# Taking the float32 splits of weights and tokens off GpSimd in a two-layer trunk

## The chip, the cores and the metric

The kernel runs on one core of one Trainium2 chip. The metric is the device time of one execution in microseconds (us); a kernel is described by the median of several executions. One more execution is taken with the hardware profiler, and every duration below comes from that one. TensorE is PE in the rows, VectorE DVE, ScalarE ACT, GpSimd POOL, SyncE SP.

## The reference, cut to what matters

Two trunk layers, each followed by a SwiGLU feed-forward. Layer 0 mixes tokens by latent attention (MLA) and by gated linear attention (GLA) side by side; layer 1 is a convolution module with 31 taps and a layer norm. There are 1152 tokens of width 1024, all in float32.

```python
def modulate(x, g, shift, scale):          # ahead of every sub-layer
    return rmsnorm(x, g) * (1 + scale) + shift

def ffn(h):                                # after every layer, hidden width 2816
    return (silu(h @ w_gate) * (h @ w_up)) @ w_down

# gla_scan, per chunk: q, k scaled by exp of the cumulated log decay
o = scores @ v + (q * exp(cum)) @ state
# conv module: h @ w_pw1, GLU, depthwise 31 taps, layernorm, silu, @ w_pw2
```

## The kernel before

Tokens lie along the free axis, features on the 128 partitions. The tokens form four tiles of 280 to 296 columns; tiles 0 and 1 make the group GA, tiles 2 and 3 the group GB, and the stages of the two groups are interleaved so that one group's feed-forward (the matmuls) covers the other group's convolution or norm.

**Splits.** TensorE takes a rounded float32 (fp32r). To keep the accuracy each operand is held as H, a rounded copy, and L, the rest. `split` (L155) makes H by a ScalarE copy (L156) and then L = source - H (L157), on VectorE unless another engine is given. `mm3` (L159) then spends three matmuls on a product: H of the weight by H of the token tile (L161), H by L (L162), L of the weight by H (L163). The last needs the weight's L, `wL`, the second the token tile's, `hL`.

**Weights.** `wtile` (L412) takes three buffers each of `wraw`, `wH` and `wL`, starts the load on SP's queue and splits it. A weight tile is 128x1024 for gate, up and the convolution's products, and 128x512 or narrower for w_down. The counter `self.wn` and the stage's entry of `WPOOL = (0, 3, 3, 0, 0)` send every third weight tile's L to GpSimd in two kinds of stage: in GA's first feed-forward, and from the moment the convolution's taps are queued (`conv_taps`, L1275) until the layer norm that follows.

**Tokens.** `affine` (L375), the last step of `modulate`, has two forms that alternate over the 8 blocks of 128 features. One uses ScalarE and VectorE directly (L390, L391); the other is `mode` 1, which multiplies on VectorE (L381), applies shift and scale on ScalarE (L383) and splits with L on GpSimd (L384). `layer_norm` splits its odd blocks with L on GpSimd (L1305). Ahead of `affine`, `x_stats` sums squares on VectorE (`ssum`, L373), and TensorE turns the sum into a row for all partitions (L188).

**Linear attention.** In `gla_b` ScalarE writes exponentials into a tile `kq` for two halves f of the heads (L904, L911). Each `kq` is then multiplied by `gqk` in two parts: the first (L913, 128x896) on VectorE for f = 0 and on GpSimd for f = 1, the second (L915, 128x1152) on VectorE for both. TensorE reads the products at L928.

**Beside it.** The convolution's taps are 31 dependent multiply-adds of some 575 or 592 columns for each of 8 blocks and each group, all on VectorE. They are pinned in their own order and dripped a few at a time between feed-forward tiles. VectorE also multiplies the gate product (`ev`, L448), splits it (`aL`), adds the result to x (L409), and sums the conditioning rows (`ada`, L292). Attention's probabilities are split with L (`pL`) on GpSimd for every fourth key block (L1233).

**Order.** A tile scheduler decides each engine's program order from the dependences and its own costs; then each engine runs its queue strictly in order.

Of the kernel before, what the change touches and what calls it, by code (L numbers as in the profile page):

```python
# [18 lines left out]
P = 128  # L19
# [12 lines left out]
W_STEP = 18  # L32
QA, Q0, Q_STEP = 3, 1, 6
FOLD = 512
WPOOL = (0, 3, 3, 0, 0)
A2 = 60
AK, MODS0 = 6, (0, 1) * 3 + (0, 0)
WB = 3, 3, 3
# [29 lines left out]
def segs(tt, w):  # L68
    return [(0, P, 0), (P, w, 1)] if tt == 0 else [(0, w, 1)]
# [47 lines left out]
class Trunk:  # L117
    def __init__(self, tc, A, O):
        self.tc, self.nc, self.A, self.O = tc, tc.nc, A, O
        self.n = 0  # L120
        self.ps = None
        self.pend = deque()
        self.ada_bank = "m"
        self.wn = self.wpool = 0
        self.sw = 512
        self.ada_pin = False
        self.adq = self.nc.sync
# [248 lines left out]
    def affine(self, tt, k, x, bc, H, L, sh, a, mode):  # L376
        nc = self.nc
        w = x.shape[1]
        if mode:
            u, y = self.tmp()[:, :w], self.tmp()[:, :w]  # L380
            nc.vector.tensor_mul(u, x, bc)  # L381
            for s, e, g in segs(tt, w):
                nc.scalar.activation(y[:, s:e], u[:, s:e], AF.Identity, bias=sh[:, k, g:g + 1], scale=a[:, k, g:g + 1])  # L383
            self.split(H[:, k, :], L[:, k, :], y, nc.gpsimd)  # L384
            return
        t = self.tmp()[:, :w]
        for s, e, g in segs(tt, w):
            nc.vector.scalar_tensor_tensor(t[:, s:e], x[:, s:e], a[:, k, g:g + 1], bc[:, s:e],
                                           op0=ALU.mult, op1=ALU.mult)
            nc.scalar.activation(H[:, k, s:e], t[:, s:e], AF.Identity, bias=sh[:, k, g:g + 1])  # L390
            nc.vector.scalar_tensor_tensor(L[:, k, s:e], t[:, s:e], sh[:, k, g:g + 1], H[:, k, s:e].bitcast(F32),  # L391
                                           op0=ALU.add, op1=ALU.subtract)
# [17 lines left out]
                                                X[tt][:, o, s:e], op0=ALU.mult, op1=ALU.add)  # L410

    def wtile(self, src):  # L412
        self.wn += 1
        eng = self.nc.gpsimd if self.wpool and self.wn % self.wpool == 0 else None
        n = src.shape[1]
        raw = self.t(self.wp, [P, KD, P], "wraw", WB[0])[:, :n]
        self.nc.sync.dma_start(raw, src)
        H = self.t(self.wp, [P, KD, P], "wH", WB[1], F32R)[:, :n]
        L = self.t(self.wp, [P, KD, P], "wL", WB[2], F32R)[:, :n]
        self.split(H, L, raw, eng)  # L420
        return H, L

    def drip(self, n):
# [132 lines left out]
    def layer0_mix(self):  # L556
        nc, A, tc = self.nc, self.A, self.tc
# [175 lines left out]
            X.update(xs)  # L733
            self.xg = getattr(self, "xg", []) + [x]
        hs = {}
        self.wpool = WPOOL[0]
        for grp in (GA, GB):
            if grp is GB:
                mx = {tt: self.h_tiles(tt, T1[tt][1] - T1[tt][0]) for tt in GB}
# [133 lines left out]
    def gla_b(self, t):  # L873
        nc, kg, S, tb = self.nc, self.kg, self.S, self.gb
        fs, bs = kg[:, 0:1024], kg[:, 1024:2048]
        NL = len(LEVELS)
        tok = slice(t * P, (t + 1) * P)
        gqk = self.t(tb, [P, 4, P], "gqk", 2)
# [12 lines left out]
        for f in range(2):  # L891
            kq = self.t(tb, [P, 2 * NL + 2, P], "kq", 3)
            for d in range(2):
                src = fs if d == 0 else bs
                for half in range(2):
                    E = self.bank("g")
                    for i, L in enumerate((laH, laL)):
                        nc.tensor.matmul(E, L[:, d * 256 + f * P:d * 256 + (f + 1) * P],
                                         src[:, half * 512:half * 512 + 512], start=(i == 0), stop=(i == 1))
                    for q in range(4):  # L900
                        l = half * 4 + q
                        iv = E[:, q * P:(q + 1) * P]
                        if l == NL:
                            nc.scalar.activation(kq[:, 2 * NL + d, :], iv, AF.Exp)  # L904
                            continue
                        s = LEVELS[l]
                        base = kq[:, l, :] if d == 0 else kq[:, l, s:]
                        st = NL * P + s if d == 0 else NL * P - s
                        ov = bass.AP(base.tensor, base.offset,
                                     [list(base.ap[0]), [st, 2], [2 * s, 64 // s], [1, s]])  # L910
                        nc.scalar.activation(ov, iv.rearrange("p (a b c) -> p a b c", a=2, c=s), AF.Exp)  # L911
                    yield
            (nc.gpsimd if f else nc.vector).tensor_mul(kq[:, 0:NL], kq[:, 0:NL], gqk[:, f, :].unsqueeze(1).to_broadcast([P, NL, P]))  # L913
            yield
            nc.vector.tensor_mul(kq[:, NL:], kq[:, NL:],  # L915
                                 gqk[:, 2 + f, :].unsqueeze(1).to_broadcast([P, NL + 2, P]))
            KQ.append(kq)
            yield
# [341 lines left out]
    def conv_taps(self, u, f, outs):  # L1260
        nc = self.nc
        n = outs[-1][1] + outs[-1][0].shape[1]
        ys, pin = [], self.tc.keep_in_program_order

        def tap(i):
            c = self.cvw[:, f, i:i + 1]
            if i == 0:
                ys.append(self.t(self.up, [P, max(UA, UB) - 2 * CPAD], "y")[:, :n])
            y = ys[0]
            if i == 0:  # L1270
                pin(nc.vector.tensor_scalar(y, u[:, 0:n], c, self.b_dw[:, f:f + 1], op0=ALU.mult, op1=ALU.add))
            else:
                for d, o in outs if i == CW - 1 else [(y, 0)]:
                    w = d.shape[1]
                    pin(nc.vector.scalar_tensor_tensor(d, u[:, i + o:i + o + w], c, y[:, o:o + w],  # L1275
                                                       op0=ALU.mult, op1=ALU.add))
        self.pend.extend(lambda i=i: tap(i) for i in range(CW))
        self.wpool = WPOOL[2]

    def layer_norm(self, C, tts):  # L1280
        nc = self.nc
        us = {}
        for tt in tts:
            c = C[tt]
            w = c.shape[2]
            ssum = self.t(self.tp, [P, self.sw], "ssum", 2)[:, :w]
            nc.vector.tensor_add(ssum, c[:, 0], c[:, 1])
            for f in range(2, KD):
                nc.vector.tensor_add(ssum, ssum, c[:, f])
            mu = self.bank()[:, :w]  # L1290
            nc.tensor.matmul(mu, self.onesd, ssum, start=True, stop=True)
            s2 = self.t(self.tp, [P, self.sw], "ssum", 2)[:, :w]
            for f in range(KD):
                nc.vector.tensor_sub(c[:, f], c[:, f], mu)
                sq = s2 if f == 0 else self.tmp()[:, :w]
                nc.scalar.activation(sq, c[:, f], AF.Square)
                if f:
                    nc.vector.tensor_add(s2, s2, sq)
            bc = self.bcast_rstd(s2, w)
            H, L = self.h_tiles(tt, w)  # L1300
            for f in range(KD):
                y = self.tmp()[:, :w]
                nc.vector.tensor_mul(y, c[:, f], bc)
                nc.scalar.activation(y, y, AF.Silu, bias=self.ln_b[:, f:f + 1], scale=self.ln_g[:, f:f + 1])
                self.split(H[:, f], L[:, f], y, nc.gpsimd if f % 2 else nc.vector)  # L1305
            us[tt] = (H, L)
        return us

# [44 lines left out]
    def layers(self, X, hs):  # L1353
        nc, A = self.nc, self.A
        pa = self.pool("act")
        self.wpool = WPOOL[1]
        NB = max(C0A + C0B + C1A + C1B)
        cut = lambda ns: list(zip(np.cumsum((0,) + ns).tolist(), ns))
        chunks = cut(C0A)
# [12 lines left out]
            if f0 == chunks[1][0]:  # L1372
                hs.update(self.modulate(X, 0, 1, GB))
        self.adp.release()
        self.wpool = 0
        gate = self.par[1][2]
        nc.vector.tensor_mul(self.bg, gate, self.b_pw2.unsqueeze(2).to_broadcast([P, KD, 2]))
        w2 = A["conv_w_pw2"][0].rearrange("(k p) f -> p k f", p=P)
# [8 lines left out]
        for c in chunks[1:-1]:  # L1387
            self.ffn(X, hs, 0, GB, *c, pa, NB, R_FF0)
        self.drip(10 ** 6)
        self.wpool = WPOOL[3]  # L1390
        us = self.layer_norm(C, GA)
        self.ffn(X, hs, 0, GB, *chunks[-1], pa, NB)
        X2 = {}
# [8 lines left out]
        for c in chunks[:-2]:  # L1402
            self.ffn(X2, h2, 1, GA, *c, pa, NB, R_FF1)
        self.drip(10 ** 6)
        self.wpool = WPOOL[3]
        us = self.layer_norm(C, GB)
        self.x_load(X2, GB)
        self.ffn(X2, h2, 1, GA, *chunks[-2], pa, NB)
# [1 line left out]
        h2.update(self.modulate(X2, 1, 1, GB))  # L1410
        self.ffn(X2, h2, 1, GA, *chunks[-1], pa, NB)
        self.store_y(X2, GA)
        self.wpool = WPOOL[4]
        self.up.release()
        for c in cut(C1B):
            self.ffn(X2, h2, 1, GB, *c, pa, NB)
# [57 lines left out]
```

## Time and profile before

| | |
|---|---|
| median of 3 executions | 3096.03 us (3094.78 to 3100.07) |
| the profiled execution, its own time | 3098.96 us |
| its span in the trace | 3097.2 us |
| TensorE busy | 97% of the span |
| VectorE busy | 70% |
| ScalarE busy | 40% |
| GpSimd busy | 13% |
| mean granted TensorE clock | 0.984 |

The span is the time between the first and the last traced instruction; 1.8 us of the profiled execution lie outside it. Where TensorE is busy all the time, only an instruction that TensorE has to wait for can change the end.

### The profile page before, as it was taken

To read this page: it belongs to the slowest core of one execution; us is meant where nothing else is said; L and a number is where in the kernel's file an instruction comes from. 1 tells how busy PE (TensorE), PEld (TensorE's weight loads), DVE (VectorE), ACT (ScalarE), POOL (GpSimd) and SP (SyncE) were. 2 spreads that over 40 slices of the span, in tenths; PEclk is the share of its full clock that TensorE was granted. 3 is DMA by queue.
4 is the path that set the end of the run, shared out by engine and by line. 5 is a ranking of instruction groups with operands and counts; after the bars stand their busy time and mean duration, and the time that the engine had idled before them with its cause. 6 is when DMAs were issued, how large, how long until landed. Compare 5 with 4: busy or idle time off the path is not lost.

```text
span 3097.2 us, 53660 instructions
## 1 busy us (share of the span) xinstructions
PE 3002.1 (97%) x21044; PEld 2813.7 (91%) x21044; DVE 2169.4 (70%) x4110; ACT 1232.1 (40%) x2652; POOL 405.2 (13%) x371
## 2 busy tenths in 40 slices
PE   7999999999989999999999999999999999999999
PEld 4999866666769999999999999999999999999998
DVE  6668478788769999634679996667888875433343
ACT  5323377566664333223422223562222255222222
POOL 1012121112120111111111110111111010000000
PEclk9999999999999999999999999999999999999999
DMA  7545522111164555423232222522322231322222
GB/s 266 169 120 149 156 88 70 55 46 52 26 188 151 168 157 155 127 82 103 80 86 83 78 82 76 149 69 83 89 86 86 83 113 51 110 82 83 81 86 78
DMA packets 449631, 320.46 MB, mean 103 GB/s; under 512 B 29646, under 2 KB 413907, under 8 KB 449378
## 3 DMA queue, kind: packets, MB, share of 16 engines
q1 hardware_dynamic: 411726, 271.06, 29.3%
q0 software_dynamic: 8944, 30.68, 3.1%
q10 hardware_dynamic: 28708, 15.29, 1.7%
q8 instruction: 166, 2.72, 0.4%
q14 instruction: 87, 0.71, 0.1%
HBM read 278.30 MB, written 38.67 MB: 102 GB/s over the span
## 4 chain that ended last, share of the span: by engine, by line
PE 75%; DVE 13%; ACT 5%; DMA 3%; issue 3%; POOL 0%; SPq 0%; ACTq 0%; DVEq 0%; POOLq 0%
PE ps_a L161 16%; PE ps_a L163 16%; PE ps_a L162 16%; PE ps_d L162 3%; PE ps_d L163 3%; PE ps_d L161 3%; DVE y L1275 2%; PE ps_g L928 2%; PE ps_a L538 2%; PE ps_a L540 2%; PE ps_a L539 2%; DVE ada L292 1%; DVE wL L157 1%; DVE x L409 1%; PE ps_c L1236 1%
## 5 line engine op out<-in xcount | busy, mean ns | idle before, releaser
L163 PE MATMUL ps_a<-hH,wL 128*128 128x288 f32 (+2 forms) x3328 | 985.3, 296 | 6.7 <-DVE wL L157 6.7
L161 PE MATMUL ps_a<-hH,wH 128*128 128x288 f32 (+2 forms) x3328 | 983.9, 296 | 1.8 <-ACT wH L156 1.8
L162 PE MATMUL ps_a<-hL,wH 128*128 128x288 f32 (+2 forms) x3328 | 985.2, 296 | 0.0
L156 ACT CAST wH<-wraw 128x1024 fp32r<-128x1024 f32 (+3 forms) x432 | 362.4, 843 | 768.4 <-PE ps_a L162 480.7
L163 PEld LDWEIGHTS ps_a<-hH,wL 128*128 128x128 f32 x3328 | 627.7, 189 | 8.0 <-DVE wL L157 7.8
L161 PEld LDWEIGHTS ps_a<-hH,wH 128*128 128x128 f32 x3328 | 629.0, 189 | 2.6 <-ACT wH L156 2.3
L162 PEld LDWEIGHTS ps_a<-hL,wH 128*128 128x128 f32 x3328 | 627.5, 189 | 0.2
L157 DVE TENSOR_TENSOR wL<-wraw,wH 128x1024 fp32r<-128x1024 f32 (+3 forms) x349 | 336.0, 965 | 130.2 <-ACT wH L156 129.3
L1275 DVE SCALAR_TENSOR_TENSOR y<-u,cvw,y 128x575 f32<-128x575 f32 (+1 forms) x464 | 420.1, 905 | 8.4
L157 POOL TENSOR_TENSOR wL<-wraw,wH 128x1024 fp32r<-128x1024 f32 (+2 forms) x83 | 172.7, 2081 | 975.3 <-ACT wH L156 975.1
L161 PE MATMUL ps_a<-aH,wH 128*128 128x288 f32 (+2 forms) x880 | 259.8, 296 | 0.2 <-ACT wH L156 0.2
L163 PE MATMUL ps_a<-aH,wL 128*128 128x288 f32 (+2 forms) x880 | 259.0, 295 | 0.0
L162 PE MATMUL ps_a<-aL,wH 128*128 128x288 f32 (+2 forms) x880 | 258.9, 294 | 0.0
L448 DVE TENSOR_TENSOR ev<-ev,ps_a 128x288 f32<-128x288 f32 (+2 forms) x176 | 79.3, 450 | 226.9 <-PE ps_a L163 225.6
L292 DVE SCALAR_TENSOR_TENSOR ada<-ada,scc,ada 128x512 f32<-128x512 f32 (+1 forms) x364 | 219.7, 647 | 20.0 <-DMA ada<-in_w_ada 19.8
L156 ACT CAST aH<-ev 128x288 fp32r<-128x288 f32 (+2 forms) x176 | 75.9, 431 | 330.7 <-DVE ev L448 329.1
L161 PEld LDWEIGHTS ps_a<-aH,wH 128*128 128x128 f32 x880 | 165.9, 189 | 0.5 <-ACT wH L156 0.5
L162 PEld LDWEIGHTS ps_a<-aL,wH 128*128 128x128 f32 x880 | 166.1, 189 | 0.0
L163 PEld LDWEIGHTS ps_a<-aH,wL 128*128 128x128 f32 x880 | 165.5, 188 | 0.5 <-DVE wL L157 0.5
L161 PE MATMUL ps_d<-aH,wH 128*128 128x288 f32 (+2 forms) x528 | 158.3, 300 | 6.3 <-ACT wH L156 3.5
L161 PE MATMUL ps_d<-hH,wH 128*128 128x288 f32 (+2 forms) x512 | 153.2, 299 | 8.6 <-DVE dr L1248 6.6
L409 DVE SCALAR_TENSOR_TENSOR x<-ps_a,par,x 128x288 f32<-128x288 f32 (+5 forms) x300 | 128.5, 450 | 45.8 <-PE ps_a L163 45.1
(338 smaller groups left out, 5770.7 us busy)
## 6 DMA issues: line engine op xcount, KB each, us to landing
wraw<-in_ffn_w_gate SPq DMA_DIRECT2D x88, 512.0 KB
wraw<-in_ffn_w_up SPq DMA_DIRECT2D x88, 512.0 KB
wraw<-in_ffn_w_down SPq DMA_DIRECT2D x144, 256.0 KB
ada<-in_w_ada SPq DMA_DIRECT2D x112, 256.0 KB
wraw<-in_conv_w_pw SPq DMA_DIRECT2D x48, 512.0 KB
in<-in_w_ada SPq DMA_DIRECT2D x8, 1024.0 KB
ada<-in_w_ada SPq DMA_DIRECT2D x64, 128.0 KB
wraw<-in_w_out SPq DMA_DIRECT2D x16, 512.0 KB
```

The source lines that it names most:

```text
L156: self.nc.scalar.copy(H, src)
L157: (eng or self.nc.vector).tensor_sub(L, src, H.bitcast(F32))
L161: mm(out, WH, hH, start=start, stop=False)
L162: mm(out, WH, hL, start=False, stop=False)
L163: mm(out, WL, hH, start=False, stop=stop)
L292: ins = self.nc.vector.scalar_tensor_tensor(acc[v], w, s, acc[v], op0=ALU.mult, op1=ALU.add)
L409: self.nc.vector.scalar_tensor_tensor(X[tt][:, o, s:e], src[:, s:e], gate[:, o, g:g + 1], X[tt][:, o, s:e], op0=ALU.mult, op1=ALU.add)
L448: nc.vector.tensor_mul(pr, sl, bu)
L538: mm(b[:, :wd], hh, wh, start=(k == 0), stop=False)
L539: mm(b[:, :wd], hh, wl, start=False, stop=False)
L540: mm(b[:, :wd], hl, wh, start=False, stop=(k == KD - 1))
L1275: pin(nc.vector.scalar_tensor_tensor(d, u[:, i + o:i + o + w], c, y[:, o:o + w], op0=ALU.mult, op1=ALU.add))
```

## The change

Every `split` in `wtile`, `affine` and `layer_norm` and the first multiply of both `kq` run on VectorE. `WPOOL` and its counter are gone. Attention's `pL` and `vL` and the memsets stay on GpSimd, and so do its DMA starts.

```diff
-WPOOL = (0, 3, 3, 0, 0)
...
     def affine(self, tt, k, x, bc, H, L, sh, a, mode):
...
-            self.split(H[:, k, :], L[:, k, :], y, nc.gpsimd)
+            self.split(H[:, k, :], L[:, k, :], y)
             return
...
     def wtile(self, src):
-        self.wn += 1
-        eng = self.nc.gpsimd if self.wpool and self.wn % self.wpool == 0 else None
...
-        self.split(H, L, raw, eng)
+        self.split(H, L, raw)
...
-            (nc.gpsimd if f else nc.vector).tensor_mul(kq[:, 0:NL], kq[:, 0:NL], gqk[:, f, :].unsqueeze(1).to_broadcast([P, NL, P]))
+            nc.vector.tensor_mul(kq[:, 0:NL], kq[:, 0:NL], gqk[:, f, :].unsqueeze(1).to_broadcast([P, NL, P]))
...
     def layer_norm(self, C, tts):
...
-                self.split(H[:, f], L[:, f], y, nc.gpsimd if f % 2 else nc.vector)
+                self.split(H[:, f], L[:, f], y)
...
     def layers(self, X, hs):
-        self.wpool = WPOOL[1]
...
-        self.wpool = 0
```

The scheduler orders the queues anew. Three places on VectorE show how; the lines are those of each kernel's own file (L1270, L444, L155, L908, L910, L926, L389 and L371 of the changed one are L1275, L448, L157, L913, L915, L931, L391 and L373 of the one before). The numbers in the names are buffers and tiles.

**Taps beside a feed-forward tile** (`y` is a tap's running sum, `ev` and `aL` the gate product and its split, `wL_19406` an up weight). Before:

```order
L1289 TENSOR_TENSOR ssum_21613<-ssum_21613,x_3598_17228 128x280
L448 TENSOR_TENSOR ev_19322<-ev_19321,ps_a_19272 128x288
L157 TENSOR_TENSOR aL_3849_19326<-ev_19322,aH_3848_19325 128x288
L1275 SCALAR_TENSOR_TENSOR y_19257<-u_3658_17758,cvw_90,y_19257 128x575 x4
L157 TENSOR_TENSOR wL_19406<-wraw_19403,wH_19405 128x1024
L1275 SCALAR_TENSOR_TENSOR y_19257<-u_3658_17758,cvw_90,y_19257 128x575
L448 TENSOR_TENSOR ev_19385<-ev_19384,ps_a_19335 128x288
```

Now:

```order
L444 TENSOR_TENSOR ev_19322<-ev_19321,ps_a_19272 128x288
L155 TENSOR_TENSOR aL_3849_19326<-ev_19322,aH_3848_19325 128x288
L1270 SCALAR_TENSOR_TENSOR y_19257<-u_3658_17758,cvw_90,y_19257 128x575 x3
L155 TENSOR_TENSOR wL_19406<-wraw_19403,wH_19405 128x1024
L1270 SCALAR_TENSOR_TENSOR y_19257<-u_3658_17758,cvw_90,y_19257 128x575 x2
L444 TENSOR_TENSOR ev_19385<-ev_19384,ps_a_19335 128x288
L155 TENSOR_TENSOR wL_19538<-wraw_19535,wH_19537 128x1024
```

`wL_19406` now stands behind three taps where it stood behind four, and `wL_19538`, a split of the next feed-forward tile that was GpSimd's, is the last row, behind the next `ev`.

**Linear attention** (`kq_5841` is the tile of the second half of the heads; the other rows belong to attention). Before:

```order
L931 TENSOR_TENSOR pt_1315_5939<-ps_g_5941,diag_966_4716 128x256
L1205 TENSOR_TENSOR mhl_6168<-mneg_5820,mhl_6168 128x9
L157 TENSOR_TENSOR pL_6296<-p_6293,pH_6295 128x512
L915 TENSOR_TENSOR kq_5841<-kq_5841,gqk_5683 128x1152
L931 TENSOR_TENSOR pt_1316_5940<-ps_g_5942,diag_966_4716 128x256
L933 COPY_PREDICATED pt_1315_5939<-mask_4714,ps_g_5941 128x256
```

Now:

```order
L926 TENSOR_TENSOR pt_1315_5939<-ps_g_5941,diag_966_4716 128x256
L1200 TENSOR_TENSOR mhl_6168<-mneg_5820,mhl_6168 128x9
L155 TENSOR_TENSOR pL_6296<-p_6293,pH_6295 128x512
L908 TENSOR_TENSOR kq_5841<-kq_5841,gqk_5683 128x896
L910 TENSOR_TENSOR kq_5841<-kq_5841,gqk_5683 128x1152
L926 TENSOR_TENSOR pt_1316_5940<-ps_g_5942,diag_966_4716 128x256
```

The first multiply (128x896), which stood on GpSimd's queue, stands directly ahead of the second.

**A modulate of the convolution layer, the end of one token tile and the sums of the next** (`hL_3482` is the first tile's L, `ssum_16709` the next tile's sum of squares). Before:

```order
L388 SCALAR_TENSOR_TENSOR tmp_16695<-x_2459_10214,par_13_82,ps_m_16647 128x160
L381 TENSOR_TENSOR tmp_16702<-x_2459_10214,ps_m_16647 128x288
L391 SCALAR_TENSOR_TENSOR hL_3482_16652<-tmp_16695,par_12_81,hH_3481_16651 128x128
L391 SCALAR_TENSOR_TENSOR hL_3482_16652<-tmp_16695,par_12_81,hH_3481_16651 128x160
L448 TENSOR_TENSOR ev_16917<-ev_16916,ps_a_16867 128x288
L373 TENSOR_TENSOR ssum_16709<-ssum_16709,tmp_16711 128x288
L373 TENSOR_TENSOR ssum_16709<-ssum_16709,tmp_16714 128x288
```

Now:

```order
L155 TENSOR_TENSOR hL_3482_16652<-tmp_16689,hH_3481_16651 128x288
L389 SCALAR_TENSOR_TENSOR hL_3482_16652<-tmp_16695,par_12_81,hH_3481_16651 128x128
L389 SCALAR_TENSOR_TENSOR hL_3482_16652<-tmp_16695,par_12_81,hH_3481_16651 128x160
L155 TENSOR_TENSOR wL_16933<-wraw_16930,wH_16932 128x1024
L155 TENSOR_TENSOR hL_3482_16652<-tmp_16703,hH_3481_16651 128x288
L371 TENSOR_TENSOR ssum_16709<-ssum_16709,tmp_16711 128x288
L371 TENSOR_TENSOR ssum_16709<-ssum_16709,tmp_16714 128x288
```

Two splits that GpSimd had and one weight's L now stand among the last rows ahead of `ssum`; before, none of them did.

## Rows read from the trace of the kernel before

**Rows 1.** The page's first part: busy time of each engine over the span.

```profile
PE 3002.1 (97%) x21044; PEld 2813.7 (91%) x21044; DVE 2169.4 (70%) x4110; ACT 1232.1 (40%) x2652; POOL 405.2 (13%) x371
```

**Rows 2.** Windows A:B: length, busy of PE, PEld, DVE, ACT, POOL, PE clock, DMA.

```profile
1625.00:1875.00 250.00, 243.64 (x1821) 241.96 (x1821) 237.50 (x330) 62.44 (x108) 36.45 (x23) 0.99 0.28 81
2200.00:2500.00 300.00, 299.63 (x2329) 299.29 (x2328) 264.98 (x412) 82.51 (x139) 40.28 (x19) 1.00 0.29 84
```

**Rows 3.** Waits of PE: line, releaser, total us, times, longest us.

```profile
PE ps_m L188 <- DVE ssum L373: 8.7, 7, 3.1
PE ps_a L163 <- DVE wL L157: 6.7, 4, 2.1
...
PE ps_g L928 <- DVE kq L915: 4.5, 4, 1.6
...
PE ps_d L163 <- DVE wL L157: 2.2, 2, 1.4
...
PE ps_a L540 <- DVE hL L391: 0.6, 1, 0.6
```

**Rows 4.** Line L157, GpSimd: count, duration ns min/median/max, first and last start, forms.

```profile
L157 POOL TENSOR_TENSOR wL<-wraw,wH x83: 1002/2383/3690, 1011.0 to 2452.5; 128x1024 fp32r<-128x1024 f32 x46, 128x512 fp32r<-128x512 f32 x32, 128x384 fp32r<-128x384 f32 x5
L157 POOL TENSOR_TENSOR hL<-tmp,hH x73: 769/815/1736, 50.8 to 2634.0; 128x288 fp32r<-128x288 f32 x32, 128x280 fp32r<-128x280 f32 x16, 128x296 fp32r<-128x296 f32 x16, 128x512 fp32r<-128x512 f32 x3
```

**Rows 5.** VectorE's groups by form, whole span: busy us, mean ns; idle before.

```profile
L157 DVE TENSOR_TENSOR wL<-wraw,wH 128x1024 fp32r<-128x1024 f32 x194 | 237.3, 1223 | 105.1 <-ACT wH L156 104.6
...
L157 DVE TENSOR_TENSOR wL<-wraw,wH 128x512 fp32r<-128x512 f32 x112 | 77.4, 696 | 20.2 <-ACT wH L156 19.8
```

**Rows 6.** VectorE, lines L157, L913, L915 and L1275, columns as in the fourth group.

```profile
L157 DVE TENSOR_TENSOR aL<-ev,aH x176: 434/457/2425, 1026.5 to 3064.6; 128x288 fp32r<-128x288 f32 x88, 128x280 fp32r<-128x280 f32 x44, 128x296 fp32r<-128x296 f32 x44
...
L157 DVE TENSOR_TENSOR hL<-tmp,hH x16: 442/452/468, 1941.1 to 2530.9; 128x280 fp32r<-128x280 f32 x8, 128x296 fp32r<-128x296 f32 x8
...
L913 DVE TENSOR_TENSOR kq<-kq,gqk x9: 1075/1083/1093, 498.8 to 856.2; 128x896 f32<-128x896 f32 x9
...
L915 DVE TENSOR_TENSOR kq<-kq,gqk x18: 1342/1486/3267, 499.8 to 863.8; 128x1152 f32<-128x1152 f32 x18
...
L1275 DVE SCALAR_TENSOR_TENSOR y<-u,cvw,y x464: 797/819/3011, 1529.9 to 2484.4; 128x575 f32<-128x575 f32 x78, 128x592 f32<-128x592 f32 x77
```

**Rows 7.** Groups by form, 1625 to 1875 us, GpSimd and then VectorE.

```profile
L157 POOL TENSOR_TENSOR wL<-wraw,wH 128x1024 fp32r<-128x1024 f32 x9 | 23.3, 2592 | 90.2 <-ACT wH L156 90.2
L157 POOL TENSOR_TENSOR wL<-wraw,wH 128x512 fp32r<-128x512 f32 x8 | 12.6, 1572 | 81.3 <-ACT wH L156 81.3
...
L1275 DVE SCALAR_TENSOR_TENSOR y<-u,cvw,y 128x575 f32<-128x575 f32 x174 | 160.1, 920 | 2.9
...
L157 DVE TENSOR_TENSOR aL<-ev,aH 128x288 fp32r<-128x288 f32 x26 | 15.2, 585 | 8.7 <-ACT aH L156 8.7
```

**Rows 8.** Timeline 1706 to 1720 us: start, duration, engine, line, count [idle before].

```profile
1711.53 5.56 DVE L1275 SCALAR_TENSOR_TENSOR y<-u,cvw,y 128x575 f32<-128x575 f32 x4
...
1714.10 2.38 POOL L157 TENSOR_TENSOR wL<-wraw,wH 128x1024 fp32r<-128x1024 f32 x1 [4.61 <-ACT wH L156]
...
1717.02 1.21 DVE L157 TENSOR_TENSOR wL<-wraw,wH 128x1024 fp32r<-128x1024 f32 x1
...
1718.29 0.40 PE L163 MATMUL ps_a<-hH,wL 128*128 128x288 f32 x1 [1.83 <-DVE wL L157]
```

**Rows 9.** Timeline 716.5 to 722 us, in linear attention.

```profile
717.05 2.09 POOL L913 TENSOR_TENSOR kq<-kq,gqk 128x896 f32<-128x896 f32 x1 [0.65 <-ACT kq L911]
...
717.17 3.18 DVE L915 TENSOR_TENSOR kq<-kq,gqk 128x1152 f32<-128x1152 f32 x1
...
720.50 0.46 PE L928 MATMUL ps_g<-kq 64*128 64x128 f32 x2 [1.53 <-DVE kq L915]
```

**Rows 10.** Windows behind two waits of PE, columns as in the second group.

```profile
2079.00:2083.00 4.00, 3.79 (x22) 3.82 (x23) 1.27 (x3) 1.32 (x2) 0.00 (x0) 0.59 0.33 92
721.00:731.00 10.00, 10.00 (x32) 6.56 (x34) 6.44 (x12) 4.11 (x9) 3.46 (x3) 0.51 0.27 68
```

More of the change, by code (lines that the diff above doesn't have):

```diff
@@ L123, in __init__ @@
         self.ada_bank = "m"
-        self.wn = self.wpool = 0
         self.sw = 512
@@ L735, in layer0_mix @@
         hs = {}
-        self.wpool = WPOOL[0]
         for grp in (GA, GB):
@@ L1277, in conv_taps @@
         self.pend.extend(lambda i=i: tap(i) for i in range(CW))
-        self.wpool = WPOOL[2]
     def layer_norm(self, C, tts):
@@ L1389, in layers @@
         self.drip(10 ** 6)
-        self.wpool = WPOOL[3]
         us = self.layer_norm(C, GA)
@@ L1404, in layers @@
         self.drip(10 ** 6)
-        self.wpool = WPOOL[3]
         us = self.layer_norm(C, GB)
@@ L1412, in layers @@
         self.store_y(X2, GA)
-        self.wpool = WPOOL[4]
         self.up.release()
```

## The prediction

> **What bounds the kernel now.** I read the busy shares first, then TensorE's waits, then the stages, then single waits in the timeline. TensorE is busy for 3002 of 3097 us, so at most the rest can be won without changing its matmuls; VectorE is busy for 70% and GpSimd for 13% [rows 1]. The share of VectorE is an average: in the two stretches that hold most convolution taps it is 237.5 of 250 us and 265 of 300 us, while TensorE is busy for 243.6 and 299.6 [rows 2]. There both queues are nearly full. The list of TensorE's waits names this change's lines: 6.7 + 2.2 us for a weight's L, 8.7 us for the sum of squares of a modulate, 4.5 us for the second multiply of `kq`, 0.6 us for a token tile's L in the first stage [rows 3]. All of them wait for VectorE, none for a GpSimd split.
>
> The next question is why VectorE was late. In the timeline at 1711 us four taps take 5.56 us, where the median tap is 0.82 us; three taps at 0.82 leave 3.1 us for the fourth. GpSimd starts a weight split at 1714.10, and both end close to 1716.5 to 1717. The weight split that VectorE has queued behind that tap ends at 1718.2, and TensorE has waited 1.83 us for it [rows 6, 8]. The split that GpSimd was doing belonged to a later tile. So GpSimd did not take work off VectorE there: while it ran for 2.4 us, VectorE's tap stood still. Linear attention shows the same: GpSimd's multiply starts at 717.05 and takes 2.09 us, VectorE's L915, started 0.12 us later, takes 3.18 us where the shortest takes 1.34, and TensorE waits 1.53 us for it [rows 6, 9]. Taps reach 3.01 us and `aL`, with a median of 0.46 us, 2.43 us [rows 6].
>
> The Trainium skill has a rule on this, in "SBUF — State Buffer", section "SBUF: two separate sides": VectorE and GpSimd share a pair of ports, which is locked for a whole instruction and blocks the other engine. The rows at 1714 and at 717 us agree. By that rule alone each moved instruction frees VectorE for GpSimd's whole duration, some 2.4 us for a price of 1.2; the sum below takes the smaller gain that the stretched rows show.
>
> **What the change adds to VectorE.** GpSimd's weight splits are 46 of 1024 columns, 32 of 512 and 5 of 384 [rows 4]. At VectorE's 1.223 and 0.696 us [rows 5] they are 46 x 1.223 + 32 x 0.696 = 78.5 us, and the five narrow ones at no more than 0.696 add 3.5: 82 us. The token splits are 73, of which 64 have 280 to 296 columns [rows 4]; at 0.452 [rows 6] these are 28.9 us. Nine of 256 to 512 columns belong to the first stage; at 0.45 to 0.70 they are 4 to 6 us. The nine multiplies of the second head half at 1.083 [rows 6] are 9.7 us. Together about 126 us of VectorE.
>
> **What it takes away.** The stretch between 1625 and 1875 us has all its terms in rows. Added: 9 splits x 1.223 + 8 x 0.696 = 16.6 us. Freed: 174 taps at 0.920 instead of 0.819 us are 17.6 us, 26 `aL` at 0.585 instead of 0.457 are 3.3 us [rows 5 to 7], together 20.9. So VectorE's load there does not rise, although it gets 17 more instructions; it even falls by 4 us. The same holds for `kq`: the pair of second-half multiplies took about 3.2 us at 717 us and should take 1.08 + 1.34 = 2.4 us. On the stretches with few taps the stretching is smaller and load is added, but there VectorE has idle time that TensorE's matmuls cover.
>
> **The path, term by term, against the profiled 3098.96 us.**
>
> *Weight splits, -7.* TensorE waits 8.9 us for them in 6 waits [rows 3]. Where such a wait looks like the one at 1718 us it should go: in the new order three taps (2.5 us) and the split (1.22 us) follow `aL`, which ends near 1711.5, so the split is done near 1715.3, ahead of TensorE's need at 1716.5. I take 7 of the 8.9 us. Bounds: 8.9 and nothing.
>
> *Clock behind them, -2.* Behind a wait at 2079 us the granted clock is 0.59 over 4 us, so 1.6 us of matmul time are lost [rows 10]; it falls from 2.4 to 1.2 GHz for part of that window. The wait at 1718 us alone costs 1.83. One such drop and a bit go with the waits. Bounds: 0 and 6 x 1.6 = 9.6.
>
> *Linear attention, -3.* Each of the nine pairs gets about 0.8 us shorter; the four waits of 4.5 us [rows 3] lose 4 x 0.8 = 3.2. Bounds: 0 and 4.5.
>
> *Clock in linear attention, -5.* Behind the wait at 720.5 us the clock is 0.51 for the next 10 us with TensorE busy throughout [rows 10]: about 5 us of work lost. The waits for `kq` are 4, so up to four such stretches could go; only rows behind one of them stand here, and I count one. Bounds: 0 and 20.
>
> *Modulates, 0.* Four of eight token splits per tile now stand in VectorE's queue ahead of the next tile's `ssum`, 4 x 0.45 = 1.8 us, and in the order shown a weight split of 1.2 us as well. Against that goes the stretching, up to the 2 us of one GpSimd split. Queued behind these are the row of L188 on TensorE, and through it the matmuls behind it in TensorE's queue. Bounds: the 8.7 us of these 7 waits gone, or 7 x 1.8 = 12.6 more.
>
> *First stage, +1.5.* TensorE already waits 0.6 us for a token split by L391 [rows 3]; nine splits of 4 to 6 us come into the same queue, and about a quarter of that reaches TensorE. Bounds: 0 and 6.
>
> *New waits, +3.* With the queue rearranged, two of the 83 weight splits that had an engine of their own may come late behind taps, at 8.9 / 6 = 1.5 us each. Bounds: 0 and the rival below.
>
> *ScalarE, SP and GpSimd's own queue, 0.* ScalarE's copies, TensorE's matmuls and the loads stay in number. GpSimd's DMA starts only lose what stood ahead of them.
>
> The sum is -12.5 us: 3086.5 against the profiled execution. That one lies 2.9 us above the median of the runs, 3096.03, for which the sum would be 3083.5; I take 3085, between the two; the rivals are placed in the same way, 1.5 us below their sum.
>
> **The rivals.**
>
> *A, slower: VectorE's single queue makes weight splits late.* Until now a third of them could run whenever GpSimd was free, in any order against the taps; now each one stands behind what the scheduler put ahead of it, and the tap stretches have only 250 - 237.5 = 12.5 us and 35 us of idle VectorE [rows 2]. A late split costs 1.5 us of wait and in about half of the cases 1.6 us of clock, 2.3 us in all. Four new ones eat the gain of the feed-forward stages; nine (of 83), with no gain there, give 9 x 2.3 = 20.7 against -3 - 5 + 1.5 = -6.5 from the rest, +14: near 3111. For it: 96% and more of TensorE and 95% of VectorE busy at once. Against it: the load in that stretch falls by my rows, and in the one place shown the split moves ahead of a tap.
>
> A sentence of the Trainium skill speaks on this side too: "Perfetto Trace Analysis", section "Optimizing Scalar/DVE Operations", says that with VectorE saturated, offloading even to GpSimd may make sense, though the shared port may spoil it. VectorE's 95% is such a case; the 3.01-us taps are the spoiling.
>
> *B, no difference.* The waits move rather than go: matmuls come behind another late operand (ScalarE's wH, `ssum`, `pL`), and the half-speed stretches of attention stay. Terms: -7 + 3 + 1.5, and modulates at +2: about -1, near 3097. For it: 3002 of 3097 us are matmuls; the waits that the change addresses are 22.7 us, 0.7% of the time [rows 1, 3].
>
> *C, a larger gain.* All wL and kq waits go (-13.4), two modulate waits go with the stretching (-4), and two half-speed stretches of attention vanish (-10), and the first stage costs its 1.5: -26, near 3071. For it: the clock falls only behind waits in the rows. Against: GpSimd keeps `pL` and `vL` in attention, so VectorE is still blocked there at times.
>
> That the change should not do what it says can be excluded but for that remainder: the order lists show the splits on VectorE.
>
> **How the numbers follow.** About 0.2% of 3096 us, 6.2 us, can be told from no change. Forecast 0.43, A 0.20, B 0.25, C 0.12. The forecast's own range is 3077 to 3093, so nearly all of it is faster by over 0.2% (0.41); C is faster (0.12); B gives 0.03 faster, 0.18 within, 0.04 slower; A gives 0.03 within and 0.17 slower; the forecast gives 0.02 within. Faster 0.56, same 0.23, slower 0.21. The range from 3068 to 3107 takes in the forecast, B, most of C and half of A.
>
> **What would show it.** Right: taps with a maximum near 0.85 us and a mean near 0.82 instead of 0.92; L915 near 1.35 us throughout; VectorE's busy time between 2150 and 2240 us; GpSimd below 150 us; the waits "L163 <- wL" under 3 us and "L928 <- kq" under 2. The forecast is wrong if the taps stay long (then something else than GpSimd blocks them), if the waits for wL or ssum grow past 18 us together (rival A), or if the attention stretch has the same clock as before while the waits for `kq` have gone.

## The result, and the profile after

The changed kernel takes 3070.34 us (3066.96 to 3076.25), the kernel before beside it 3095.41: a ratio of 0.9919, with a 95% interval of 0.9905 to 0.9933. That is 25 us, somewhat over twice the 11 us that the forecast of 3085 meant, inside its range near the lower end, and close to rival C's 3071. Later executions of the same kernel gave 3073.76 us and 0.9921 (0.9905 to 0.9938). The bound of 0.2% named in the prediction is clearly passed. Three executions, of 4106, 4807 and 15541 us, are left out of all that follows; the one of 4807 us is the only traced one of the change without its token part, which so has a time here and no rows.

The page's first part for the changed kernel:

```profile
PE 2984.5 (97%) x21044; PEld 2800.8 (91%) x21044; DVE 2172.0 (71%) x4275; ACT 1237.5 (40%) x2652; POOL 143.0 (5%) x206
```

Set beside [rows 1]: VectorE has 165 instructions more and is busy for the same time, 2172.0 against 2169.4 us. GpSimd lost 262 us of work, and VectorE paid nothing for it in sum. TensorE runs the same 21044 matmuls in 17.6 us less of busy time, so not only its waits have shrunk. The statement ahead of the change that only an instruction that TensorE has to wait for can change the end left this out, and so did the prediction's first bound, that at most TensorE's idle rest can be won.

TensorE's waits after the change (line, releaser, total us, times, longest):

```profile
PE ps_a L161 <- DVE wL L155: 5.4, 7, 1.4
PE ps_a L159 <- ACT ev L443: 4.6, 1, 4.6
...
PE ps_a L159 <- DVE ev L444: 2.8, 2, 2.3
...
PE ps_d L161 <- DVE wL L155: 1.4, 4, 0.4
...
PE ps_m L186 <- DVE ssum L371: 1.1, 3, 0.6
```

Against [rows 3], the wait for `kq` by DVE has left the list, `ssum` fell from 8.7 to 1.1 us, the weight splits only from 8.9 to 6.8, and 7.4 us of waits for `ev` (L443, ScalarE's SiLU of the gate, and L444, VectorE's product) are new.

Where VectorE's time went: taps and `aL` by form between 1625 and 1875 us, as in [rows 7], after the change.

```profile
L1270 DVE SCALAR_TENSOR_TENSOR y<-u,cvw,y 128x575 f32<-128x575 f32 x155 | 126.2, 814 | 2.1
...
L155 DVE TENSOR_TENSOR aL<-ev,aH 128x288 fp32r<-128x288 f32 x26 | 11.8, 456 | 6.5 <-ACT aH L154 6.5
```

A mean tap takes 0.814 us instead of 0.920, a mean `aL` 0.456 instead of 0.585. The changed kernel is some 27 us ahead there, so the window does not hold the same work (155 taps against 174), and only the means can be compared.

The two multiplies of `kq` and the taps over the whole span (duration ns min/median/max, first and last start):

```profile
L908 DVE TENSOR_TENSOR kq<-kq,gqk x18: 1075/1084/1635, 499.2 to 847.9; 128x896 f32<-128x896 f32 x18
...
L910 DVE TENSOR_TENSOR kq<-kq,gqk x18: 1344/1352/1354, 500.2 to 848.9; 128x1152 f32<-128x1152 f32 x18
...
L1270 DVE SCALAR_TENSOR_TENSOR y<-u,cvw,y x464: 804/823/840, 1502.9 to 2454.3; 128x575 f32<-128x575 f32 x78, 128x592 f32<-128x592 f32 x77
```

No tap is now longer than 0.84 us in the whole kernel, and L915's counterpart L910 takes 1.34 to 1.35 us in all 18 cases, where [rows 6] had 1.34 to 3.27. The timeline at the place of [rows 8]:

```profile
1684.17 2.52 DVE L1270 SCALAR_TENSOR_TENSOR y<-u,cvw,y 128x575 f32<-128x575 f32 x3
1686.61 1.22 DVE L155 TENSOR_TENSOR wL<-wraw,wH 128x1024 fp32r<-128x1024 f32 x1
```

Three taps and the split, as the order showed; TensorE's 1.83 us wait at this place is gone: from 1680 to 1700 us it waits for nothing.

The stages split the gain. One window holds attention, from its first `pL` to the feed-forward's first `wL`; the second holds all that follows (length, busy of PE, PEld, DVE, ACT, POOL, mean PE clock, DMA share, GB/s). Before:

```profile
382.00:902.00 520.00, 485.84 (x2519) 349.44 (x2517) 395.52 (x809) 342.17 (x921) 108.26 (x97) 0.94 0.22 67
902.00:3097.00 2195.00, 2158.31 (x16184) 2143.26 (x16184) 1523.14 (x2588) 748.07 (x1340) 242.53 (x188) 0.99 0.34 100
```

After:

```profile
384.00:883.00 499.00, 469.25 (x2517) 338.16 (x2515) 386.96 (x813) 342.29 (x918) 83.80 (x88) 0.98 0.23 68
883.00:3068.00 2185.00, 2155.50 (x16184) 2139.60 (x16184) 1531.46 (x2740) 752.27 (x1343) 14.10 (x41) 0.99 0.34 101
```

Attention is 21 us shorter, the rest 10 us, and what lies ahead of attention is 2 us longer. In attention TensorE's idle time, length less busy, went from 34.2 to 29.8 us: 4.4 us. The other 16.6 us are busy time of the same matmuls. They passed faster because the mean granted clock rose from 0.94 to 0.98.

Two places show most of it. Before, TensorE waits 1.5 us for `kq` at 720 us and 1.6 us at 774 us, and behind both the clock falls by half: from 721 to 731 us [rows 9, 10] and from 776 to 790 us. The second (length, TensorE's busy time, clock, DMA share, GB/s):

```profile
776.00:786.00 10.00, 10.00 (x44) 0.50 0.00 0
```

After, some 11 us earlier in time, the clock is full around both places:

```profile
707.00:712.00 5.00, 5.00 (x29) 1.00 0.07 15
712.00:722.00 10.00, 8.86 (x54) 1.00 0.54 153
...
757.00:767.00 10.00, 10.00 (x55) 1.00 0.18 52
767.00:777.00 10.00, 9.73 (x65) 1.00 0.07 15
777.00:787.00 10.00, 10.00 (x57) 1.00 0.12 38
```

These 24 us at half clock are 12 of the 16.6 us.

### The profile page after: what moved, and what is told of

Read it like the earlier page. It is cut to its first block, busy times and chain, and to the rows that moved or that the text cites. A ratio compares the mean times of both kernels' runs of the same rounds, so it can differ in the third digit from the quotient of the medians.

```text
span 3068.5 us, 53591 instructions
## 1 busy us (share of the span) xinstructions
PE 2984.5 (97%) x21044; PEld 2800.8 (91%) x21044; DVE 2172.0 (71%) x4275; ACT 1237.5 (40%) x2652; POOL 143.0 (5%) x206
## 4 chain that ended last, share of the span: by engine, by line
PE 80%; DVE 7%; ACT 6%; DMA 4%; issue 2%; POOL 0%; SPq 0%; ACTq 0%; DVEq 0%; POOLq 0%
PE ps_a L161 18%; PE ps_a L159 18%; PE ps_a L160 17%; PE ps_d L159 4%; PE ps_d L161 4%; PE ps_d L160 4%; PE ps_g L923 2%; DVE ada L290 1%; PE ps_c L1231 1%; PE ps_a L534 1%; PE ps_p L1193 1%; PE ps_a L535 1%; PE ps_a L536 1%; ACT kq L906 1%; DVE wL L155 1%
## 5 line engine op out<-in xcount | busy, mean ns | idle before, releaser
L155 DVE TENSOR_TENSOR wL<-wraw,wH 128x1024 fp32r<-128x1024 f32 (+3 forms) x432 | 415.6, 964 | 149.1 <-ACT wH L154 148.0
L1270 DVE SCALAR_TENSOR_TENSOR y<-u,cvw,y 128x575 f32<-128x575 f32 (+1 forms) x464 | 381.7, 823 | 7.8
L444 DVE TENSOR_TENSOR ev<-ev,ps_a 128x288 f32<-128x288 f32 (+2 forms) x176 | 79.6, 452 | 219.3 <-PE ps_a L161 218.9
L290 DVE SCALAR_TENSOR_TENSOR ada<-ada,scc,ada 128x512 f32<-128x512 f32 (+1 forms) x364 | 209.5, 622 | 20.7 <-DMA ada<-in_w_ada 20.5
L161 PE MATMUL ps_d<-aH,wL 128*128 128x288 f32 (+2 forms) x528 | 155.1, 296 | 1.4 <-DVE wL L155 1.4
```

Source lines behind the costliest of these rows:

```text
L155: (eng or self.nc.vector).tensor_sub(L, src, H.bitcast(F32))
L161: mm(out, WL, hH, start=False, stop=stop)
L290: ins = self.nc.vector.scalar_tensor_tensor(acc[v], w, s, acc[v], op0=ALU.mult, op1=ALU.add)
L444: nc.vector.tensor_mul(pr, sl, bu)
```

## The experiments

Every kernel was timed with the kernel before beside it on the same chip; ratios are to that, with 95% intervals.

### One part at a time

**Only the `kq` multiplies** (kernel before, one line):

```diff
-            (nc.gpsimd if f else nc.vector).tensor_mul(kq[:, 0:NL], ...
+            nc.vector.tensor_mul(kq[:, 0:NL], ...
```

> The kernel before with only the nine multiplies of linear attention (kq, second head half) moved to VectorE. Theory: GpSimd's multiply stops VectorE's next one, TensorE waits for that, and its clock drops behind the waits; all of this lies in the attention stretch, so this edit alone brings the larger part of the 25 us: 14 to 20 us faster, near 3078. L915 takes 1.35 us in all 18 cases, the four waits of L928 for kq L915 are gone, and the half-speed stretches at 720 to 732 and 773 to 788 us with them. Rival (chance clock): the clock in attention falls at other places as often as before, and the edit is worth the 4.5 us of waits or less: 3091 or more. Rival (order): the gain comes from weight splits that reach TensorE earlier, and this edit is within 3 us of the kernel before.

Measured: 3080.28 us, ratio 0.9950 (0.9935 to 0.9965), some 15 us, as expected.

**Only the weight splits:**

```diff
-WPOOL = (0, 3, 3, 0, 0)
+WPOOL = (0, 0, 0, 0, 0)
```

> The kernel before with only the 83 weight splits moved to VectorE. Theory: taps drop to at most 0.85 us, VectorE's load in 1625 to 1875 us falls, TensorE's waits for wL fall, 6 to 10 us faster, near 3087; attention is as before (the first feed-forward matmul at 901 to 902 us). Rival (single queue): VectorE's queue gets the splits late, no faster than before or slower, 3095 to 3105. Rival (parts do not add): with kq left on GpSimd the scheduler's order differs, and the sum of the parts misses the whole by over 6 us.

Measured: 3086.52 us, 0.9970 (0.9956 to 0.9984), some 9 us. In two points the expectation missed. Attention, which this edit does not touch, ended at 893 us and not at 901 to 902. And TensorE's waits for weight splits did not fall, from 8.9 us; they rose to 10.4:

```profile
PE ps_a L163 <- DVE wL L157: 8.5, 8, 3.3
...
PE ps_d L163 <- DVE wL L157: 1.9, 5, 0.5
```

What fell behind attention are the waits for `ssum`, from 8.7 to 4.7 us, and TensorE's busy time, by 5 us.

**Only the token splits** (the lines of `affine` and `layer_norm` in the change's diff):

> The kernel before with only the token splits (73 in affine and in layer_norm) moved to VectorE. Theory: small either way; the first stage gets 1 to 2 us longer, the modulates gain or lose up to 3 us: 3090 to 3098. Rival: the waits for ssum (8.7 us) were caused by GpSimd's token splits, and they go: 3083 to 3088.

Measured: 3099.03 us, 1.0009 (0.9995 to 1.0023): no difference, on the slow side.

**The change without `kq`** (the first diff, backwards, on the changed kernel):

> The changed kernel with the nine kq multiplies back on GpSimd. Theory: it loses what the first run gains, 14 to 20 us, so near 3087, and the waits of L928 for kq come back with the half-speed stretches behind them. Rival (chance clock): within 5 us of the changed kernel, 3066 to 3076.

Measured: 3086.35 us, 0.9974 (0.9963 to 0.9986), and the waits for `kq` are back:

```profile
PE ps_g L923 <- DVE kq L910: 4.5, 4, 1.6
```

**The change without its token part** (`kq` and weights):

> The change without its token part: kq and the weight splits on VectorE, the splits of affine and layer_norm as before on GpSimd. Theory (the parts add): 15 + 9 us faster than the kernel before and about as fast as the whole change, 3067 to 3073; the token part is worth nothing or costs a little. Rival (token splits on GpSimd block VectorE as the weights did): 3 us or more slower than the changed kernel.

Measured: 3070.45 us, 0.9906 (0.9891 to 0.9921), with the changed kernel beside it at 3073.76:

> The changed kernel again, beside the others of this call: 3066 to 3076 as measured before.

The parts add: -0.50, -0.30 and +0.09% are -0.71%, and the whole is -0.81 (+-0.14); each part has an interval as wide, so the two agree. The stage windows put each in its place. Attention with `kq` alone, then with weights alone:

```profile
383.00:880.00 497.00, 468.06 (x2515) 337.77 (x2513) 386.36 (x813) 342.52 (x918) 83.59 (x88) 0.98 0.22 68
880.00:3079.00 2199.00, 2158.07 (x16184) 2141.83 (x16184) 1524.95 (x2593) 750.28 (x1343) 243.36 (x188) 0.99 0.34 101
```

```profile
381.00:893.00 512.00, 478.17 (x2517) 345.49 (x2515) 396.21 (x808) 342.51 (x921) 108.64 (x97) 0.95 0.22 68
893.00:3080.00 2187.00, 2153.24 (x16184) 2138.66 (x16184) 1521.78 (x2672) 750.31 (x1340) 74.80 (x105) 0.99 0.34 101
```

The change without `kq`, attention:

```profile
383.00:900.00 517.00, 484.16 (x2522) 349.65 (x2519) 395.75 (x808) 342.93 (x923) 108.66 (x97) 0.94 0.22 67
```

And tokens alone:

```profile
390.00:905.00 515.00, 481.62 (x2519) 346.71 (x2516) 395.90 (x808) 342.51 (x921) 108.73 (x97) 0.94 0.22 67
905.00:3099.00 2194.00, 2157.68 (x16184) 2144.41 (x16184) 1536.10 (x2653) 749.72 (x1340) 188.97 (x124) 0.99 0.34 100
```

In these traces and both of the changed kernel attention takes 497 to 499 us with `kq` on VectorE and 512 to 520 with it on GpSimd; the 8 us among the latter show how much it varies without any edit there. With the weight splits on VectorE the rest takes 2183 to 2187 us, otherwise 2194 to 2199. What the token splits do behind attention, 2194 against 2195 us, is not clear of the variation.

The guess of chance clock fails for `kq`. In all four traces with it on GpSimd TensorE waits 4.5 to 5.3 us for it, 1.5 us of that at 712 to 724 us and 1.6 at 764 to 777, and within 3 us of each of these two the clock falls by half, for 6 to 10 and for 14 to 20 us. None of the three with it on VectorE waits for it; one half-speed stretch of 7 us, near 775 to 780 us, is left in two of them. That the scheduler's order alone brings the gain is not excluded by these runs, since it changes with every edit; but each part brings its gain in the stage that it touches, whatever the other parts do.

### Is it blocking, or waiting for GpSimd's result?

GpSimd subtracts a second time for the same 83 weight tiles, and no engine needs its result:

```diff
         self.split(H, L, raw)
+        if twice:
+            self.nc.gpsimd.tensor_sub(raw, raw, H.bitcast(F32))
```

> The changed kernel, and in addition GpSimd subtracts again for the same 83 weight tiles, in place in the raw weights, which nothing reads after that; VectorE's own splits stay, so nothing waits for GpSimd's result except the reuse of the raw buffer. Theory (GpSimd blocks VectorE): taps get their 2 to 3 us cases back, the mean tap rises from 0.82 to about 0.90 us, VectorE's busy time rises by 50 to 100 us, and 9 us or more of the gain are lost, since VectorE now has both the splits and the blocking: 3079 to 3095. Rival (the gain came from not waiting behind GpSimd's queue, or from the scheduler's order): the taps stay at 0.82 and the time at the changed kernel's 3070, within 4 us.

Measured: 3109.12 us, 1.0036 (1.0022 to 1.0050): 35 us above the changed kernel beside it, slower than the kernel before, and above the range expected. VectorE is busy for 2250.7 us instead of 2172.0. Its taps, whole span:

```profile
L1277 DVE SCALAR_TENSOR_TENSOR y<-u,cvw,y 128x592 f32<-128x592 f32 x232 | 209.8, 904 | 4.0
L1277 DVE SCALAR_TENSOR_TENSOR y<-u,cvw,y 128x575 f32<-128x575 f32 x232 | 209.1, 901 | 3.8
```

They are back at the 0.9 us of [rows 7], and the stage behind attention takes 2219 us, while attention itself stays at 499. Nothing waits for these instructions but the reuse of the raw buffer, so the stretching is blocking. For `kq` no such run was made: there the blocking rests on L915, which took 1.34 to 3.27 us where GpSimd had its multiply and takes 1.34 to 1.35 without it. To bound the buffer's share, the same with a one-operand instruction, which holds the buffer longer:

```diff
-            self.nc.gpsimd.tensor_sub(raw, raw, H.bitcast(F32))
+            self.nc.gpsimd.tensor_scalar(raw, raw, 1.0, None, op0=ALU.mult)
```

> As the run in which GpSimd subtracts again for 83 weight tiles (3109), but GpSimd's extra instruction has one operand: it multiplies the raw weights by 1.0 in place. Theory (any GpSimd instruction that reads and writes this memory stops VectorE's two-operand ones, for as long as it runs): taps are stretched in proportion to its duration; if it takes half as long as the subtraction, half of the 36 us, 3080 to 3095. Rival (only a GpSimd instruction with two operands stops VectorE): mean tap 0.82 us and 3068 to 3076.

Measured: 3082.99 us, 0.9950 (0.9937 to 0.9962), 9 to 13 us above the changed kernel: in the theory's range, but not by its reason, since the instruction takes longer and not half as long. GpSimd's extra instructions with two operands, then with one, and the taps beside the latter:

```profile
L422 POOL TENSOR_TENSOR wraw<-wraw,wH 128x1024 f32<-128x1024 f32 x46 | 124.4, 2704 | 805.7 <-DVE wL L157 739.8 <-ACT tmp L372 65.9
```

```profile
L422 POOL TENSOR_SCALAR wraw<-wraw 128x1024 f32<-128x1024 f32 x46 | 140.2, 3048 | 787.6 <-DVE wL L157 708.6 <-ACT tmp L372 65.9 <-issue 13.1
...
L1277 DVE SCALAR_TENSOR_TENSOR y<-u,cvw,y 128x592 f32<-128x592 f32 x232 | 197.7, 852 | 4.0
```

It runs longer, 3.05 against 2.70 us, yet stretches the 592-column tap by 0.02 us (0.831 in the changed kernel) instead of 0.07. So of the 35 us some 9 to 13 can come from the buffer and this milder stretching together, as far as this run tells; the rest is the two-operand instruction stopping VectorE. TensorE's waits for ScalarE's copies of weights, where a late load would show, agree: 3.8 us in the changed kernel, 5.5 with one operand, 6.3 with two.

### Why did nine multiplies bring 15 us?

The changed kernel with one more pass of VectorE over the same part of `kq`, no GpSimd:

```diff
+            if f:
+                nc.vector.tensor_scalar(kq[:, 0:NL], kq[:, 0:NL], 1.0, None, op0=ALU.mult)
```

> The changed kernel with one more pass of VectorE over the second head half's first part of kq (times 1.0, 128x896), nine times, between the two multiplies. No GpSimd is added. Theory (it is the lateness of kq that costs, through TensorE's waits and the half clock behind them, whoever causes it): waits of L923 for kq come back with half-speed stretches in attention, 6 to 14 us slower than the changed kernel, 3076 to 3084, though only 9 us of VectorE are added beside an engine that is idle for a fifth of that stage. Rival (GpSimd's blocking costs attention in more ways than through kq's lateness): within 4 us, 3067 to 3075.

Measured: 3091.6 us, 0.9977 (0.9965 to 0.9990), above the range expected. Its attention:

```profile
382.00:898.00 516.00, 485.19 (x2522) 349.06 (x2521) 395.73 (x823) 344.06 (x921) 83.74 (x88) 0.95 0.22 67
```

Nine passes of 0.86 us, 7.7 us in all, undo the gain in attention, 17 us. TensorE's idle time is 30.8 us, 1 us more than in the changed kernel; its busy time is 485.2 instead of 469.3, at a clock of 0.95. So a delay in VectorE's queue at this place costs that much without any GpSimd, and the price is paid in clock: half speed from 721 to 731 and from 782 to 792 us. That it is the lateness of `kq` itself is not shown, since the pass delays all that stands behind it, and the waits that grew are not those for `kq`, as expected, but those for the probabilities (4.1 us in the changed kernel):

```profile
PE ps_s L1223 <- ACT p L1227: 6.3, 8, 2.5
```

The opposite direction: attention's `pL`, all on VectorE, and every second one on GpSimd instead of every fourth.

```diff
-... nc.gpsimd if kt % 4 == 0 else nc.vector)
+...)
```

> The changed kernel with the 40 splits of attention's probabilities (pL, every fourth key block) on VectorE too. Theory: 32 x 0.68 + 8 x 0.35 = 25 us are added to VectorE in attention, 10 to 15 us of stretching go, TensorE's waits for GpSimd's pL (3 us) go; attention 2 to 6 us shorter, 3064 to 3069. Rival (VectorE is the nearer bound in attention, 77% busy there): pL and the reductions come later, attention 5 us longer, 3075 or more.

Measured: 3085.68 us, 0.9957 (0.9944 to 0.9970), 12 us slower than the changed kernel; the theory fell, and the rival's number came out.

```diff
-... nc.gpsimd if kt % 4 == 0 else nc.vector)
+... nc.gpsimd if kt % 2 == 0 else nc.vector)
```

> The changed kernel with every second instead of every fourth pL of attention on GpSimd, the other way than the run that put all of them on VectorE and lost 12 us. Theory (in attention VectorE's neighbours mostly read PSUM and are not stopped, so GpSimd is real help there, but its pL takes 1.37 us and TensorE then waits for it): between 5 us faster and 5 us slower, 3066 to 3076; VectorE busy falls by 20 us. Rival (VectorE's load sets attention): 8 us or more faster, under 3063. Rival (blocking in attention as in the feed-forward): 8 us or more slower.

Measured: 3098.30 us, 1.0000 (0.9985 to 1.0014), some 25 us slower than the changed kernel; this theory fell too. Two of the twelve executions took 3084 and 3085 us, and the profiled one, 3105.12 us, lies above the median. Attention of the first, then of the second with TensorE's longest wait there:

```profile
391.00:902.00 511.00, 482.30 (x2518) 344.66 (x2516) 397.31 (x857) 342.67 (x921) 36.28 (x48) 0.94 0.23 68
```

```profile
391.00:913.00 522.00, 490.01 (x2517) 352.20 (x2515) 371.15 (x780) 338.57 (x918) 129.82 (x120) 0.95 0.21 65
...
PE ps_c L1231 <- POOL pL L155: 8.4, 15, 1.2
```

VectorE's busy time in attention went up by 10 us in one and down by 16 in the other, and both lost. So VectorE's load alone does not set this stage. In the second TensorE waits 15 times for GpSimd's `pL`. In both the clock is back at 0.94 to 0.95 with idle times of 28.7 and 32.0 us: the loss is again mostly busy time. Each has a long wait for `kq`, 1.5 us at 551 us and 1.3 us at 527, though `kq` is on VectorE, and right behind it a half-speed stretch of 14 and of 20 us. In all six traces with a wait for `kq` of 1.3 us or more, a half-speed stretch follows within 3 us.

### Could a part be taken back?

The first stage passes GpSimd as `eng`, the others nothing:

```diff
-            self.split(H[:, k, :], L[:, k, :], y)
+            self.split(H[:, k, :], L[:, k, :], y, eng)
```

> The changed kernel with only the nine token splits of the first stage (before layer 0) back on GpSimd. Theory: the first stage has no covered VectorE time for them, so attention begins 2 to 4 us earlier, as in the kernels that keep token splits on GpSimd; the rest as in the changed kernel: 3067 to 3071, 2 to 4 us under the changed kernel beside it and the fastest of all. Rival (the token splits were worth nothing anywhere): within 1 us of the changed kernel's 3070 to 3074; also a token split on GpSimd that blocks VectorE there as the weights did, 3 us slower.

Measured: 3072.18 us, 0.9917 (0.9904 to 0.9931): no difference from the change. Attention began at 385 us, the changed kernel's at 384 and 388. Over all traces it begins at 382 to 392 us with these splits on VectorE (nine) and at 381 to 385 with them on GpSimd (four), so a few us may be lost there, but the time does not show it. The first stage's splits are worth nothing that these runs can tell, and no variant here beats the change clearly; the one without token splits has the lowest ratio, 0.9906, inside the change's interval.

## Why the prediction was right, and its size too small

**The mechanism** was right: GpSimd's two-operand splits stop VectorE, so moving them costs VectorE nothing in sum. Taps, L915, the waits for `kq` and the busy time of VectorE and GpSimd came out as forecast, and the doubled subtraction shows the blocking by itself. One sign missed: the waits "L163 <- wL" were to be under 3 us and are 5.4.

**Clock in linear attention, -5 forecast: the mis-sized term.** It measured -16.6 us (485.84 to 469.25 busy); its bound of 20 held. The prediction counted one half-speed stretch of 10 us, because it had rows behind one wait only. The second long wait for `kq` had 14 us at half speed behind it, and both went, which is 12 us; the rest lies in shorter stretches. The extra pass shows that such stretches also come without a listed wait for `kq`, so counting these waits is not a full account of the term either.

**Linear attention's waits, -3:** all 4.5 us of waits for `kq` went, and the stage has 4.4 us less idle time.

**Feed-forward: the sum came near by luck, its terms were not right.** Forecast were -7 (weight splits), -2 (clock), 0 (modulates), +3 (new waits), together -6; the stage gained 10. The waits for weight splits fell by 2.1 only, those for `ssum` by 7.6, new waits for `ev` brought 7.4; busy time fell by 2.8. The weight splits removed the wait at [rows 8] as computed, but others came late behind taps in the single queue, as in rival A, in 11 shorter waits of at most 1.4 us; with the weights alone these waits even grew. The step that failed for `ssum` is the one that set 1.8 us of token splits against a 2-us stretch and took them as equal: with both parts on VectorE the sums came in time. Weights alone left 4.7 us of it and tokens alone 4.2, so each part removes about half; by which instruction stays open. The new waits for `ev` go with the token splits: 0.7 and 2.8 us stand in the trace with these alone, 4.6 and 2.8 with the weight splits beside them, none in the traces where GpSimd kept the token splits. They take back what `ssum` gave, so the 0 for the modulates was right in sum, by luck.

**First stage, +1.5:** attention starts 2 us later in one trace of the changed kernel and 6 in the other, but moving these splits back did not shorten the time. The term stays within the variation.

**Rivals.** A: its mechanism exists, at a price below the gain. B fell. C came nearest in time, though by other terms: most of its excess is the attention clock.

## What to carry to other kernels

Look for instructions of the shared engine's neighbour that take a multiple of their shortest time: the sum of that stretching, not the busy share, says whether offloading helps. In a stage where TensorE's clock is not steady, price a delay by the busy time that TensorE loses and not by its wait; add a known pass at that place to learn the price. An offload that TensorE waits for may be right at one share only: here one `pL` in four on GpSimd was better than none, by 12 us, and better than two in four, by some 25.

## What the runs showed of the hardware that was not expected

**The clock falls without a wait right before it.** In the kernel with the extra pass, 5-us windows (length, TensorE's busy time, clock, DMA share, GB/s):

```profile
775.00:780.00 5.00, 4.88 (x36) 1.00 0.12 45
780.00:785.00 5.00, 5.00 (x23) 0.71 0.11 25
785.00:790.00 5.00, 5.00 (x21) 0.50 0.16 59
```

TensorE is idle for 0.12 us of these 15, and yet goes from 2.4 to 1.2 GHz. At 720 us of the kernel before it fell right behind a 1.5-us wait [rows 9, 10]. So the prediction's argument for rival C, that the clock falls only behind waits, does not hold for all rows. What sets the moment stays open.

**GpSimd's blocking depends on its operands.** A two-operand GpSimd instruction of 2.7 us stretches taps up to 2.99 us, a one-operand one of 3.0 us up to 1.61:

```profile
L1277 DVE SCALAR_TENSOR_TENSOR y<-u,cvw,y x464: 799/823/2991, 1523.2 to 2491.4; 128x575 f32<-128x575 f32 x78, 128x592 f32<-128x592 f32 x77
```

```profile
L1277 DVE SCALAR_TENSOR_TENSOR y<-u,cvw,y x464: 800/822/1610, 1515.8 to 2469.7; 128x575 f32<-128x575 f32 x78, 128x592 f32<-128x592 f32 x77
```

The Trainium skill ("SBUF — State Buffer", section "SBUF: two separate sides") lets a VectorE instruction with two operands in SBUF and a GpSimd instruction that reads SBUF exclude each other, for the whole instruction of the one that starts first. With two operands on GpSimd the rows agree; with one they do not:

```profile
1677.79 3.22 POOL L422 TENSOR_SCALAR wraw<-wraw 128x1024 f32<-128x1024 f32 x1 [13.37 <-DVE wL L157]
...
1678.29 2.06 DVE L157 TENSOR_TENSOR wL<-wraw,wH 128x1024 fp32r<-128x1024 f32 x1
...
1680.27 0.81 DVE L1277 SCALAR_TENSOR_TENSOR y<-u,cvw,y 128x575 f32<-128x575 f32 x1
```

VectorE's split starts behind GpSimd's multiply, loses 0.8 us against its usual 1.2, and ends 0.7 us ahead of it; the tap that follows runs beside the rest of the multiply in its usual 0.81 us. The measurement decides.
